# Products of transposed weight strips in two runs per block pair: all high parts, then all low parts

## The chip, the cores and the metric

The kernel runs on one core of one Trainium2 chip. The metric is the device time of one execution in microseconds (us), the median of several executions. The profile is one execution taken by the hardware profiler; its engines are PE (TensorE matmul), PEld (TensorE weight load), DVE (VectorE), ACT (ScalarE), POOL (GpSimd) and SP (SyncE).

## The reference, cut to what matters

A causal decoder trunk with two layers, 256 tokens and a width of 2048, all in float32. Layer 0 has stick-breaking attention with 16 heads; layer 1 has attention over shared keys and values in three dilated groups of four heads. Each layer then has a gated feed-forward part (up to 2 x 5632 columns, a causal convolution of width 3, SiLU gate, down to 2048) and a gated embedding:

```
x = x + mixer(rms_norm(x))                                  # w_qkv, w_o | w_q, w_kv, w_o
u = conv(rms_norm(x) @ w_up);  x = x + (silu(u[:, :D_FF]) * u[:, D_FF:]) @ w_down
x = x + sigmoid(rms_norm(x) @ w_gate) * (p @ w_proj)
```

So nearly all of the work is products of a 256-token activation with large float32 weight matrices that are each used once.

## The kernel before, in words

The stream x is kept transposed: features on the 128 partitions, 256 tokens along the free side, 16 blocks of 128 features. A weight matrix is cut into strips of 512 output columns, and a strip into K-blocks of 128 input features. One load (`L209`, on SP's queue) brings four K-blocks of a strip into a `raw` buffer (1 MB).

Precision comes from splitting each float32 number into a high part that TensorE's reduced float32 type holds exactly and a low part that is the rest. For weights ACT writes the high parts (`whi`, `L217`) and DVE the low parts (`wlo`, `L218`), two K-blocks (a block pair) at a time, into four buffers each. Activations are split the same way and stand as one tile of 512 columns: [high 256 | low 256].

`strip_t` computes four output blocks of 128 features for one strip, transposed, each in a PSUM bank of its own. Per K-block and output block it issues two matmuls on PE, each with a weight load of its own (128 x 128) ahead of it:

- the high product, H: `whi` against all 512 columns of the activation tile, into all 512 columns of the bank. Columns 0 to 255 take high x high, columns 256 to 511 high x low.
- the low product, L: `wlo` against the 256 high columns, added into columns 256 to 511.

In this text an H and its L together are a pair of products. The generator `steps` sets the order: in the first block pair of a strip by output block (so that the new strip can begin as soon as one bank is free), in the middle block by block over the four outputs, and in the last block pair by output again (so that the first output can be read while the others are still computed). In each of these places H and L alternate; only at a strip's very last K-block L stands ahead of H.

There are five such accumulator banks. When an output is complete, ACT copies the second half of its bank out (`L281`) and DVE adds the first half (`L282`), or DVE adds both halves to x (`L289`, `L290`); then the bank is free for the strip after the next output.

`strip_1` (the embedding parts) issues three products of 256 columns per output and block, without a 512-column one. `strip_v` (values) uses the activation as stationary operand and 512 columns of weights as moving one: three products of 512 columns. Both take their order from `steps` too.

A scheduler places the instructions of each engine: it keeps to the program's order where it can, and takes a later instruction first where it reckons that an earlier one would wait. The splitting of weights has a higher priority and runs ahead as far as the four buffers allow. On the chip each engine takes its instructions strictly in that order.

Of the kernel before, what the change touches and what calls it, by code (L numbers as in the profile page):

```python
# [17 lines left out]
P = 128  # L18
S = 256
# [15 lines left out]

# columns of the packed per-feature vectors
G_ATTN, G_FFN, G_PLE, G_KV, G_FIN = 0, 2 * KB, 4 * KB, 6 * KB, 7 * KB
V_CONV = 8 * KB
NVEC = V_CONV + 2 * 4 * 2 * FB
# columns of the packed constants  # L40
C_NT, C_NONE, C_ONE, C_FREQ = 0, P, 2 * P, 3 * P
# [4 lines left out]
TWO_PI = 2.0 * math.pi  # L46
NBANK = {"acc": 5, "att": 1}  # PSUM banks by use; two more are a pair of their own
MAGIC = 1.5 * 2.0 ** 23
# [15 lines left out]

RAW = 4  # K-blocks of a weight load
NRING, NRAW, NWSP = 42, 4, 4  # buffers: K-blocks, weights as loaded, weights split
AHEAD = 200  # how far in the program the splitting of weights may run ahead
LAG = 2  # blocks by which the first norm's squares trail the split
KV_AT = (0, 6, 12, 16)  # blocks split for K and V behind each of the query strips
PI_PARTS = _two_pi_parts()  # L70
# [3 lines left out]
def tile_trunk(ctx, tc, xT_d, pT_d, pos_d, vec_d, cst_d, csb_d, wqkv, wo_a, wkv, wq_b, wo_b, wup, wdn, wpg, wpp, out_d):  # L74
# [28 lines left out]

    # ---- loads of vectors, constants and the stream
    vec = cst.tile([P, NVEC], F32, name="vec")
# [22 lines left out]

    # ---- pieces
    def split_x(src, j, bases):  # L130
        """K-blocks of src * gain, split exactly: [high 256 | low 256]."""
        out = []
        for b in bases:
            h = rt("h", dt=F32R)
            nc.scalar.activation(h[:, :S], src, AF.Copy, scale=gain(b, j))
            nc.vector.scalar_tensor_tensor(  # L136
                h[:, S:], src, gain(b, j), f32(h[:, :S]), op0=OP.mult, op1=OP.subtract
            )
            out.append(h)
        return out  # L140
# [5 lines left out]
    class Norm:  # L146
        """Sum of squares over the blocks as they come, then 1/rms on every partition."""

# [6 lines left out]
        def load_table(self):  # L155
            """The table set with both Ln and Exp, behind what ACT has been given so far."""
            self.table = nc.scalar.preload_act_table_set("natural_log_exp_and_others")
            tc.keep_in_program_order(self.table)
# [40 lines left out]
    def weights(W, s, n, fine=False, before=lambda k0: None, base=0):  # L199
        """Pairs of K-blocks of a strip, split: (first block, high parts, low parts)."""  # L200
        size = 2 if fine else RAW
# [19 lines left out]
    def steps(it, n, outs, tail=2, begin=True):  # L221
        """(block, output, parts) of a strip: by output where outputs begin and in the last blocks."""
        held = []
        for k0, hi, lo in it:
            if k0 >= n - tail:
                held.append((k0, hi, lo))
            elif k0 == 0 and begin:
                yield from ((k0 + i, o, hi[:, i], lo[:, i]) for o in range(outs) for i in range(2))
            else:
                yield from ((k0 + i, o, hi[:, i], lo[:, i]) for i in range(2) for o in range(outs))  # L230
        for o in range(outs):
            yield from ((k0 + i, o, hi[:, i], lo[:, i]) for k0, hi, lo in held for i in range(2))

    def strip_t(W, s, xs, fine=False, before=lambda k0: None, base=0):
        """Four output blocks, transposed: [main | corrections] in a bank each."""
        n = len(xs)
        ps = [None] * 4
        for k, o, hi, lo in steps(weights(W, s, n, fine, before, base), n, 4, begin=not fine):
            if k == 0:
                ps[o] = bank("acc", "acc")  # L240
            c = slice(o * P, (o + 1) * P)
            if k < n - 1:
                nc.tensor.matmul(ps[o], hi[:, c], xs[k], start=k == 0, stop=False)  # L243
                nc.tensor.matmul(ps[o][:, S:], lo[:, c], xs[k][:, :S], start=False, stop=False)  # L244
            else:
                nc.tensor.matmul(ps[o][:, S:], lo[:, c], xs[k][:, :S], start=False, stop=False)  # L246
                nc.tensor.matmul(ps[o], hi[:, c], xs[k], start=False, stop=True)  # L247
        return ps

    def strip_1(W, s, xs, tail=2, two=None):  # L250
        """Four output blocks, transposed, all three products in 256 columns."""
        n = len(xs)
        ps = [None] * 2
        a = dict(skip_group_check=True)
        for k, o, hi, lo in steps(weights(W, s, n), n, 4, tail):
            if k == 0 and o % 2 == 0:
                ps[o // 2] = two[:, o // 2, :] if two is not None else bank("acc", "acc")
            c = slice(o * P, (o + 1) * P)
            d = ps[o // 2][:, (o % 2) * S : (o % 2 + 1) * S]
            nc.tensor.matmul(d, lo[:, c], xs[k][:, :S], start=k == 0 and o % 2 == 0, stop=False, **a)  # L260
            nc.tensor.matmul(d, hi[:, c], xs[k][:, S:], start=False, stop=False, **a)  # L261
            nc.tensor.matmul(d, hi[:, c], xs[k][:, :S], start=False, stop=k == n - 1, **a)  # L262
        return [ps[o // 2][:, (o % 2) * S : (o % 2 + 1) * S] for o in range(4)]

    def strip_v(W, s, xs):
        """512 output columns with the tokens on the partitions."""
        n = len(xs)
        ps = [None] * 2
        for k, t, hi, lo in steps(weights(W, s, n), n, 2):
            if k == 0:  # L270
# [29 lines left out]
    def pv(a0, a1, v, h, o):  # L300
        """o <- (weighted values)^T of a head, split. a0: keys 0 x 256, a1: keys 1 x 128."""
        po = bank("po")
# [4 lines left out]

    # ---- rotary tables: cos and signed sin on 32 partitions
    rot = cst.tile([ROT, 2, S], F32, name="rot")
# [30 lines left out]
    def rotate(t):  # L340
        """t: [128, 256] of a head, in place on its first 32 partitions."""
        sw = tt("sw", (ROT, S), tag="t", bufs=6)
# [4 lines left out]

    # ---- layer parts
    def stick_weights(q, k):
        """Weights^T of two heads a tile: keys 0 x 256 queries of each, keys 1 x 128 of each."""  # L350
        ws = []
# [63 lines left out]
    def mixer_b(hq, hkv_of, rstd, rc):  # L415
# [20 lines left out]
        for g in range(NG):  # L436
            k = project(wkv, g, hkv, None)
            gm = cbf[:, B_GM + g * S : B_GM + (g + 1) * S]
            for h in range(HG):
# [16 lines left out]
                es.append(e)  # L456
        # weights of the groups, from the softmax denominators
        lse = cst.tile([P, 2, NG, HG], F32, name="lse")
# [132 lines left out]

    # ---- the trunk
    idf = cst.tile([P, P], F32, name="idf")
# [43 lines left out]

# ---- layout on the host


def _strips(w):
    """[K, N] -> [N/512, K/512, 128, 4, 512]: four K-blocks of a strip are one run of memory."""
    k, n = w.shape
# [4 lines left out]
def _cols(v):  # L648
    """[..., n * 128] -> [128, ...*n]"""
    return np.ascontiguousarray(v.reshape(-1, P).T)  # L650
# [66 lines left out]
```

## Time and profile before

| | |
|---|---|
| median of three runs | 2414.59 us (2414.16 to 2414.65) |
| span of the profiled execution, first to last instruction | 2413.4 us, 1.2 us below the median |
| PE busy | 2390.6 us (99%), 13914 matmuls and as many weight loads |
| DVE busy | 1645.9 us (68%) |
| ACT busy | 1271.4 us (53%) |
| DMA | 439.92 MB at 182 GB/s over the span |
| chain that ended last | PE 98% |

How to read it: a matmul's row has a start and a duration, but matmuls are pipelined and the next one starts well before the duration of the one before is over. So the durations don't add up to time. What a matmul costs in a dense stretch is the distance from its start to the start of the next one, and that is what this document calls its slot. The weight load rows (PEld) start with the matmul ahead and overlap it.

### The profile page before, as it was taken

The page shows a single profiled execution, that of the slowest core. Times are in us where ns is not written, and L with a number is a line of the kernel's source. Part 1 is how long each engine was busy: PE and PEld are TensorE (multiplying, and loading weights), DVE is VectorE, ACT ScalarE, POOL GpSimd, SP SyncE. Part 2 cuts the span into 40 slices and gives each one's busy share as a digit, 9 for nine tenths or more (in the row PEclk, how much of TensorE's full clock was granted, in tenths as well). Part 3 has the DMA queues.
Part 4 walks back from the last instruction along what each step waited for, and adds up shares of the span by engine and source line. Part 5 has one row for each costly group of instructions (what it writes and reads, how often), then busy time and mean ns, then how long its engine had stood idle before and what let it go on. Part 6 is the DMA issues. An engine that isn't in the chain of part 4 may idle for free.

```text
span 2413.4 us, 34932 instructions
## 1 busy us (share of the span) xinstructions
PE 2390.6 (99%) x13914; PEld 2089.3 (87%) x13914; DVE 1645.9 (68%) x2654; ACT 1271.4 (53%) x1845; POOL 3.6 (0%) x6
## 2 busy tenths in 40 slices
PE   8999999999999999999999999999999999999997
PEld 7888888888888888888998888888888888888897
DVE  8555556777765577766778875777776557776665
ACT  6555545655543455644555444565554345555453
POOL 0000000000000000000000000000000000000000
PEclk9999999999999999999999999999999999999999
DMA  7444445555555555555555444555555555555542
GB/s 277 163 169 170 162 174 197 182 185 191 185 185 189 187 182 190 190 184 186 175 192 184 169 155 166 188 190 189 180 190 191 181 187 192 182 185 192 183 166 105
DMA packets 64004, 439.92 MB, mean 182 GB/s; under 512 B 7232, under 2 KB 7392, under 8 KB 12128
## 3 DMA queue, kind: packets, MB, share of 16 engines
q1 hardware_dynamic: 62352, 435.19, 51.1%
q10 hardware_dynamic: 1488, 2.49, 0.3%
q8 instruction: 109, 1.79, 0.3%
q14 instruction: 55, 0.45, 0.1%
HBM read 435.55 MB, written 2.10 MB: 181 GB/s over the span
## 4 chain that ended last, share of the span: by engine, by line
PE 98%; DVE 1%; ACT 1%; DMA 0%; issue 0%; DVEq 0%; SPq 0%; ACTq 0%
PE acc L243 50%; PE acc L244 25%; PE acc L247 3%; PE acc L262 2%; PE acc L261 2%; PE acc L260 2%; PE accv L274 2%; PE accv L275 2%; PE accv L276 2%; PE acc L246 2%; PE po L304 1%; ACT whi L217 0%; DVE wlo L218 0%; PE two L260 0%; PE two L261 0%; PE two L262 0%
## 5 line engine op out<-in xcount | busy, mean ns | idle before, releaser
L218 DVE TENSOR_TENSOR wlo<-raw,whi 128x1024 fp32r<-128x1024 f32 (+1 forms) x825 | 1007.6, 1222 | 677.5 <-ACT whi L217 672.4
L217 ACT ACTIVATE whi<-raw 128x1024 fp32r<-128x1024 f32 (+1 forms) x825 | 871.8, 1058 | 930.4 <-PE acc L243 691.8
L243 PE MATMUL acc<-h,whi 128*128 128x512 f32 x3480 | 1241.7, 399 | 8.6 <-DVE h L136 8.6
L244 PE MATMUL acc<-h,wlo 128*128 128x256 f32 x3480 | 977.2, 281 | 0.0
L243 PEld LDWEIGHTS acc<-h,whi 128*128 128x128 f32 x3480 | 655.2, 188 | 158.3 <-DVE h L136 8.6
L244 PEld LDWEIGHTS acc<-h,wlo 128*128 128x128 f32 x3480 | 658.2, 189 | 10.4
L243 PE MATMUL acc<-g,whi 128*128 128x512 f32 x1344 | 476.0, 398 | 0.0
L244 PE MATMUL acc<-g,wlo 128*128 128x256 f32 x1344 | 375.5, 280 | 0.0
L243 PEld LDWEIGHTS acc<-g,whi 128*128 128x128 f32 x1344 | 252.3, 188 | 58.8
L244 PEld LDWEIGHTS acc<-g,wlo 128*128 128x128 f32 x1344 | 253.7, 189 | 3.3
L243 PE MATMUL acc<-o,whi 128*128 128x512 f32 x416 | 147.9, 398 | 0.0
L262 PE MATMUL acc<-h,whi 128*128 128x256 f32 x512 | 145.3, 284 | 0.0
L260 PE MATMUL acc<-h,wlo 128*128 128x256 f32 x512 | 144.9, 283 | 0.0
L261 PE MATMUL acc<-h,whi 128*128 128x256 f32 x512 | 144.9, 283 | 0.0
L244 PE MATMUL acc<-o,wlo 128*128 128x256 f32 x416 | 115.2, 280 | 0.0
L281 ACT ACTIVATE c<-acc 128x256 f32<-128x256 f32 x232 | 86.4, 373 | 30.5 <-PE acc L247 30.5
L261 PEld LDWEIGHTS acc<-h,whi 128*128 128x128 f32 x512 | 98.2, 192 | 0.1
L262 PEld LDWEIGHTS acc<-h,whi 128*128 128x128 f32 x512 | 98.2, 192 | 0.1
L260 PEld LDWEIGHTS acc<-h,wlo 128*128 128x128 f32 x512 | 98.2, 192 | 0.1
L282 DVE TENSOR_TENSOR c<-acc,c 128x256 f32<-128x256 f32 x232 | 91.8, 416 | 0.7 <-ACT c L281 0.7
L247 PE MATMUL acc<-h,whi 128*128 128x512 f32 x232 | 92.0, 397 | 0.0
L243 PEld LDWEIGHTS acc<-o,whi 128*128 128x128 f32 x416 | 77.9, 188 | 16.0
(164 smaller groups left out, 2014.5 us busy)
## 6 DMA issues: line engine op xcount, KB each, us to landing
raw<-in_wup SPq DMA_DIRECT2D x176, 1024.0 KB, 4.8
raw<-in_wdn SPq DMA_DIRECT2D x88, 1024.0 KB, 4.8
raw<-in_wqkv SPq DMA_DIRECT2D x44, 1024.0 KB, 4.8
raw<-in_wpg SPq DMA_DIRECT2D x32, 1024.0 KB, 4.8
raw<-in_wkv SPq DMA_DIRECT2D x24, 1024.0 KB, 4.8
raw<-in_wo_a SPq DMA_DIRECT2D x16, 1024.0 KB, 4.8
raw<-in_wq_b SPq DMA_DIRECT2D x12, 1024.0 KB, 4.8
raw<-in_wo_b SPq DMA_DIRECT2D x12, 1024.0 KB, 4.8
```

The lines of the kernel that those rows point to most:

```text
L217: nc.scalar.activation(hi[:, c], r, AF.Copy)
L218: nc.vector.tensor_tensor(lo[:, c], r, f32(hi[:, c]), op=OP.subtract)
L243: nc.tensor.matmul(ps[o], hi[:, c], xs[k], start=k == 0, stop=False)
L244: nc.tensor.matmul(ps[o][:, S:], lo[:, c], xs[k][:, :S], start=False, stop=False)
L246: nc.tensor.matmul(ps[o][:, S:], lo[:, c], xs[k][:, :S], start=False, stop=False)
L247: nc.tensor.matmul(ps[o], hi[:, c], xs[k], start=False, stop=True)
L260: nc.tensor.matmul(d, lo[:, c], xs[k][:, :S], start=k == 0 and o % 2 == 0, stop=False, **a)
L261: nc.tensor.matmul(d, hi[:, c], xs[k][:, S:], start=False, stop=False, **a)
L262: nc.tensor.matmul(d, hi[:, c], xs[k][:, :S], start=False, stop=k == n - 1, **a)
L274: nc.tensor.matmul(ps[t], xl, hi, start=k == 0, stop=False)
L281: nc.scalar.activation(c, ps[:, S:], AF.Copy)
L282: nc.vector.tensor_tensor(c, ps[:, :S], c, op=OP.add)
```

## The change

`steps` now yields lists (groups) of products where it yielded single ones: a group for each output in a strip's first and last block pair, and one group of eight (four outputs, two blocks) for each block pair in the middle. `strip_t` takes a group and issues all H of it, and then all L. The last L of an output now ends its accumulation. In the very first strip of the program the first group is sorted by block. `strip_1` and `strip_v` flatten the groups; their middle block pairs now go output by output with the two blocks side by side, where they went block by block. Comments were removed as well.

```diff
     def steps(it, n, outs, tail=2, begin=True):
...
             elif k0 == 0 and begin:
-                yield from ((k0 + i, o, hi[:, i], lo[:, i]) for o in range(outs) for i in range(2))
+                for o in range(outs):
+                    yield [(k0 + i, o, hi[:, i], lo[:, i]) for i in range(2)]
             else:
-                yield from ((k0 + i, o, hi[:, i], lo[:, i]) for i in range(2) for o in range(outs))
+                yield [(k0 + i, o, hi[:, i], lo[:, i]) for o in range(outs) for i in range(2)]
         for o in range(outs):
-            yield from ((k0 + i, o, hi[:, i], lo[:, i]) for k0, hi, lo in held for i in range(2))
+            yield [(k0 + i, o, hi[:, i], lo[:, i]) for k0, hi, lo in held for i in range(2)]
 
     def strip_t(W, s, xs, fine=False, before=lambda k0: None, base=0):
...
-        for k, o, hi, lo in steps(weights(W, s, n, fine, before, base), n, 4, begin=not fine):
-            if k == 0:
-                ps[o] = bank("acc", "acc")
-            c = slice(o * P, (o + 1) * P)
-            if k < n - 1:
+        for group in steps(weights(W, s, n, fine, before, base), n, 4, begin=not fine):
+            if fine and group[0][0] == 0:
+                group.sort(key=lambda g: g[0])
+            for k, o, hi, lo in group:
+                if k == 0:
+                    ps[o] = bank("acc", "acc")
+                c = slice(o * P, (o + 1) * P)
                 nc.tensor.matmul(ps[o], hi[:, c], xs[k], start=k == 0, stop=False)
-                nc.tensor.matmul(ps[o][:, S:], lo[:, c], xs[k][:, :S], start=False, stop=False)
-            else:
-                nc.tensor.matmul(ps[o][:, S:], lo[:, c], xs[k][:, :S], start=False, stop=False)
-                nc.tensor.matmul(ps[o], hi[:, c], xs[k], start=False, stop=True)
+            for k, o, hi, lo in group:
+                c = slice(o * P, (o + 1) * P)
+                nc.tensor.matmul(ps[o][:, S:], lo[:, c], xs[k][:, :S], start=False, stop=k == n - 1)
         return ps
```

How the instructions move. The first place is PE's order for one middle block pair of a strip of the down projection (`g` are its activation blocks, `acc` the banks, 512 columns mark an H and 256 an L). Before:

```order
L243 MATMUL acc_6099<-g_6051,whi_6309 128x512
L244 MATMUL acc_6099<-g_6051,wlo_6310 128x256
L243 MATMUL acc_6104<-g_6051,whi_6309 128x512
L244 MATMUL acc_6104<-g_6051,wlo_6310 128x256
L243 MATMUL acc_6109<-g_6051,whi_6309 128x512
L244 MATMUL acc_6109<-g_6051,wlo_6310 128x256
```

And the same block pair now, up to its third L:

```order
L246 MATMUL acc_6099<-g_6051,whi_6309 128x512
L246 MATMUL acc_6099<-g_6064,whi_6309 128x512
L246 MATMUL acc_6104<-g_6051,whi_6309 128x512
L246 MATMUL acc_6104<-g_6064,whi_6309 128x512
L246 MATMUL acc_6109<-g_6051,whi_6309 128x512
L246 MATMUL acc_6109<-g_6064,whi_6309 128x512
L246 MATMUL acc_6114<-g_6051,whi_6309 128x512
L246 MATMUL acc_6114<-g_6064,whi_6309 128x512
L249 MATMUL acc_6099<-g_6051,wlo_6310 128x256
L249 MATMUL acc_6099<-g_6064,wlo_6310 128x256
L249 MATMUL acc_6104<-g_6051,wlo_6310 128x256
```

Eight H now stand in a row, and the eight L (three are shown) behind them; the two blocks of the pair go into a bank one directly behind the other.

The second place is the end of that strip and the start of the next one on PE. Before, from the last output's last three products on:

```order
L244 MATMUL acc_6114<-g_6077,wlo_6330 128x256
L246 MATMUL acc_6114<-g_6090,wlo_6330 128x256
L247 MATMUL acc_6114<-g_6090,whi_6329 128x512
L243 MATMUL acc_6363<-g_3871,whi_6359 128x512
L244 MATMUL acc_6363<-g_3871,wlo_6360 128x256
L243 MATMUL acc_6363<-g_3884,whi_6359 128x512
L244 MATMUL acc_6363<-g_3884,wlo_6360 128x256
```

Now, the same stretch:

```order
L246 MATMUL acc_6114<-g_6090,whi_6329 128x512
L249 MATMUL acc_6114<-g_6077,wlo_6330 128x256
L249 MATMUL acc_6114<-g_6090,wlo_6330 128x256
L246 MATMUL acc_6363<-g_3871,whi_6359 128x512
L246 MATMUL acc_6363<-g_3884,whi_6359 128x512
L249 MATMUL acc_6363<-g_3871,wlo_6360 128x256
L249 MATMUL acc_6363<-g_3884,wlo_6360 128x256
```

At strip ends and starts the runs are two long: H H L L for each output, where an end had H L L H and a start H L H L.

The third place lies a few rows on, where the new strip's fourth output (`acc_6378`) begins. Before, its products stood directly behind the third output's, ahead of the second block pair (`whi_6383`):

```order
L244 MATMUL acc_6373<-g_3884,wlo_6360 128x256
L243 MATMUL acc_6378<-g_3871,whi_6359 128x512
L244 MATMUL acc_6378<-g_3871,wlo_6360 128x256
L243 MATMUL acc_6378<-g_3884,whi_6359 128x512
L244 MATMUL acc_6378<-g_3884,wlo_6360 128x256
L243 MATMUL acc_6363<-g_3897,whi_6383 128x512
```

Now:

```order
L249 MATMUL acc_6373<-g_3884,wlo_6360 128x256
L246 MATMUL acc_6363<-g_3897,whi_6383 128x512
L246 MATMUL acc_6363<-g_3910,whi_6383 128x512
L246 MATMUL acc_6368<-g_3897,whi_6383 128x512
L246 MATMUL acc_6378<-g_3871,whi_6359 128x512
L246 MATMUL acc_6378<-g_3884,whi_6359 128x512
L249 MATMUL acc_6378<-g_3871,wlo_6360 128x256
```

The scheduler here took three H of the second block pair ahead of the fourth output's first product, so the second block pair's high parts are asked for four products earlier.

Over the whole program there are as many matmuls, weight loads, splits, evictions and DMAs as before. Of the 5568 H of `strip_t`, 4264 stand in middle block pairs, in runs of eight, and 1304 in strips' first and last block pairs, in runs of two; near some strip starts the scheduler made runs of five and three of them. SP's queue is unchanged; on DVE and ACT some evictions and splits change places with their neighbours.

More of the change, by code (lines that the diff above doesn't have):

```diff
@@ L254, in strip_1 @@
         a = dict(skip_group_check=True)
-        for k, o, hi, lo in steps(weights(W, s, n), n, 4, tail):
+        for k, o, hi, lo in (g for group in steps(weights(W, s, n), n, 4, tail) for g in group):
             if k == 0 and o % 2 == 0:
@@ L268, in strip_v @@
         ps = [None] * 2
-        for k, t, hi, lo in steps(weights(W, s, n), n, 2):
+        for k, t, hi, lo in (g for group in steps(weights(W, s, n), n, 2) for g in group):
             if k == 0:
```

## The prediction

> **What bounds the kernel now.** I read the page first: busy shares, granted clock, chain.
>
> ```profile
> PE 2390.6 (99%) x13914; PEld 2089.3 (87%) x13914; DVE 1645.9 (68%) x2654; ACT 1271.4 (53%) x1845; POOL 3.6 (0%) x6
> PEclk9999999999999999999999999999999999999999
> PE 98%; DVE 1%; ACT 1%; DMA 0%; issue 0%; DVEq 0%; SPq 0%; ACTq 0%
> PE acc L243 50%; PE acc L244 25%; PE acc L247 3%; PE acc L262 2%; PE acc L261 2%; PE acc L260 2%; PE accv L274 2%; PE accv L275 2%; PE accv L276 2%; PE acc L246 2%; PE po L304 1%; ACT whi L217 0%; DVE wlo L218 0%; PE two L260 0%; PE two L261 0%; PE two L262 0%
> ```
>
> The chain lies on PE for 98% of the span, and 80% of it are the lines of `strip_t` (50 + 25 + 3 + 2). The granted clock stays at nine tenths or more (1.00 in the windows below). Then PE's waits:
>
> ```profile
> PE acc L243 <- DVE h L136: 8.6, 1, 8.6
> PE nrm L176 <- ACT sq L165: 1.1, 2, 0.7
> ```
>
> The first matmul waits 8.6 us for its activation; after that hardly anything is waited for. PE is therefore bound by how fast it takes matmuls, and the change can only act through the slots of H and L, from one start to the next. How many there are, from the groups of PE kept apart by shape:
>
> ```profile
> L243 PE MATMUL acc<-h,whi 128*128 128x512 f32 x3480 | 1241.7, 399 | 8.6 <-DVE h L136 8.6
> L243 PE MATMUL acc<-g,whi 128*128 128x512 f32 x1344 | 476.0, 398 | 0.0
> L243 PE MATMUL acc<-o,whi 128*128 128x512 f32 x416 | 147.9, 398 | 0.0
> L247 PE MATMUL acc<-h,whi 128*128 128x512 f32 x232 | 92.0, 397 | 0.0
> L247 PE MATMUL acc<-g,whi 128*128 128x512 f32 x64 | 25.4, 396 | 0.0
> L247 PE MATMUL acc<-o,whi 128*128 128x512 f32 x32 | 12.7, 396 | 0.0
> ```
>
> That is 5240 + 328 = 5568 pairs of an H and an L. The mean durations (399 ns) overlap, so I don't add them; the price of a pair comes from long dense windows. Window, its length, PE busy and matmuls of L243, and below of L247, in two stretches of the up projections:
>
> ```profile
> 430.00:670.00 240.00, 227.78 (x641) 1.00 0.54 189
> 1572.00:1816.00 244.00, 231.78 (x653) 1.00 0.53 186
> ...
> 430.00:670.00 240.00, 15.88 (x40) 1.00 0.54 189
> 1572.00:1816.00 244.00, 15.88 (x40) 1.00 0.53 186
> ```
>
> 240 / 681 = 0.3524 us and 244 / 693 = 0.3521 us a pair. I take 0.3522, and for the whole 5568 x 0.3522 = 1961 us, 81% of the span, as the chain has it.
>
> **The change part by part.** It removes and adds no instruction. What it changes is the neighbours of each matmul, so I looked for what a slot costs by its neighbours. In the timeline of PE, alternating order does not have one price. Two stretches, the first and the last row of each:
>
> ```profile
> 500.06 0.40 PE L243 MATMUL acc<-h,whi 128*128 128x512 f32 x1
> 505.37 0.40 PE L243 MATMUL acc<-h,whi 128*128 128x512 f32 x1
> ...
> 1127.75 0.39 PE L243 MATMUL acc<-g,whi 128*128 128x512 f32 x1
> 1133.99 0.39 PE L243 MATMUL acc<-g,whi 128*128 128x512 f32 x1
> ```
>
> The first holds 15 pairs: 5.31 / 15 = 0.354 us. The second holds 18: 6.24 / 18 = 0.3467 us. The same two instructions alternate in both, so PE has a slow and a fast pattern of alternation. 0.3522 lies at about (0.3522 - 0.3467) / (0.354 - 0.3467) = 75% slow. Now slots without alternation, which the other two kinds of strip give. 512 columns behind 512 in `strip_v`, where the first row comes right behind two matmuls of 256:
>
> ```profile
> 227.45 0.39 PE L275 MATMUL accv<-wlo,h 128*128 128x512 f32 x1
> 229.29 0.39 PE L274 MATMUL accv<-whi,h 128*128 128x512 f32 x1
> 231.56 0.39 PE L275 MATMUL accv<-wlo,h 128*128 128x512 f32 x1
> ```
>
> The first eight slots take 1.84 us, 0.230 each; the next ten 2.27 us, 0.227 each. And 256 columns behind 256 in `strip_1`, first behind an H, then deep inside:
>
> ```profile
> 1148.58 0.28 PE L260 MATMUL acc<-h,wlo 128*128 128x256 f32 x1
> 1149.52 0.28 PE L262 MATMUL acc<-h,whi 128*128 128x256 f32 x1
> ...
> 1200.05 0.28 PE L260 MATMUL two<-p,wlo 128*128 128x256 f32 x1
> 1203.89 0.28 PE L262 MATMUL acc<-h,whi 128*128 128x256 f32 x1
> ```
>
> The first eight take 0.94 us, 0.1175 each; the 32 inside 3.84 us, 0.120 each. Settled, an H and an L cost 0.227 + 0.120 = 0.347 us, the fast pattern of alternation. Right after a switch an H is about 3 ns dearer and an L 2.5 ns cheaper, so a run of eight H behind L and a run of eight L behind H cost 1.84 + 0.94 = 2.78 us, or **0.3475 a pair**. The slow pattern shows in no run of equal matmuls.
>
> The 1304 pairs in runs of two have their nearest rows in strip ends, where L L and H H stand side by side:
>
> ```profile
> 604.41 0.28 PE L244 MATMUL acc<-h,wlo 128*128 128x256 f32 x1
> 604.53 0.28 PE L246 MATMUL acc<-h,wlo 128*128 128x256 f32 x1
> 604.65 0.40 PE L247 MATMUL acc<-h,whi 128*128 128x512 f32 x1
> 604.88 0.40 PE L243 MATMUL acc<-h,whi 128*128 128x512 f32 x1
> 606.97 0.40 PE L243 MATMUL acc<-h,whi 128*128 128x512 f32 x1
> ```
>
> From 604.88 to 606.97 there are three outputs with two pairs each: 2.09 / 6 = **0.3483 a pair**. As a circle H L L H and H H L L have the same neighbours, so I take this price.
>
> The sum: 4264 x 0.3475 + 1304 x 0.3483 = 1481.7 + 454.2 = 1935.9 us against 1961, **25.1 us less**. The profiled span of 2413.4 becomes 2388.3; with the 1.2 us by which the median lies above it, 2389.5 us.
>
> Bounds of the pair price, which no row shows in exactly the new order. From below: every pair at 0.3467 gives 1930.4, a gain of 30.6 (2384.0); if all L in the runs kept the cheap 0.1175 beside a settled H of 0.227, 0.3445, it would be 4264 x 0.0077 + 1304 x 0.0039 = 38 us (2376.7), which I hold for unlikely since the rows pay one against the other. From above: the single slots inside `strip_t` itself, L to L 0.12 (604.41 to 604.53) and H to H 0.23 (604.65 to 604.88), make 0.350: 1948.8, a gain of 12.2 (2402.4). Further up lies the slow pattern, a rival.
>
> Edits that I cost at nothing. *Buffers of the split weights*: the H of a block pair are now done eight L earlier, so ACT may refill `whi` about 8 x 0.12 = 1 us sooner; `wlo` comes free at the end of the pair as before.
>
> ```profile
> ACT whi L217 <- PE acc L243: 691.8, 434, 2.6
> DVE wlo L218 <- ACT whi L217: 672.4, 522, 5.2
> ```
>
> ACT already waits for PE, and DVE for ACT, so splitting is ahead and stays hidden; without that cover a pair of splits would cost PE the 1.2 us of a `wlo`. *Banks*: the first output of a new strip takes the fifth bank, and the fourth needs the old third one, read last by this row of DVE:
>
> ```profile
> 607.87 0.41 DVE L282 TENSOR_TENSOR c<-acc,c 128x256 f32<-128x256 f32 x1
> ...
> 609.08 0.40 PE L243 MATMUL acc<-h,whi 128*128 128x512 f32 x1
> ```
>
> It ends at 608.28, 0.8 us ahead of the fourth output. Ends and starts keep their order by output, so this margin stays, and the evictions that changed places on DVE stay within it. *First strip*: each second block's activation is needed behind one to four H instead of four pairs, about 1.2 us sooner.
>
> ```profile
> 20.77 0.47 DVE L136 SCALAR_TENSOR_TENSOR h<-x,vec,h 128x256 fp32r<-128x256 f32 x1
> ...
> 22.44 0.40 PE L243 MATMUL acc<-h,whi 128*128 128x512 f32 x1
> ```
>
> This second block is ready at 21.24, the pair starts at 22.44: still 1.2 us to spare; the 8.6 us at the start stay.
>
> **The rivals.**
>
> *A slot depends on its own columns alone.* Then order is worth nothing: 2414.6. The Trainium skill has such a rule (TensorE: Matmul & The Clock Gate, Back-to-back issue gap): a warm matmul takes N / 2.4 ns and about 2.5 ns more, 325 ns for a pair in any order. Against it stand 0.354 and 0.3467 for the same alternation, and a 512-column slot of 0.230 behind 256 columns and 0.227 later.
>
> *Single-switch prices hold.* If in short runs the 0.350 of the neighbours within `strip_t` stays, the gain is half: 2402.4. For it: these are the only rows with this code's own operands. Against: they are single slots next to an alternating stretch, and each is rounded to 10 ns.
>
> *Slower: the slow pattern takes hold of everything.* If it comes from the ratio of H to L on PE and not from the switching, and the short disorder at strip ends is what now resets it, then runs without such a reset would stand at 0.354 throughout: 5568 x 0.354 = 1971, 10 us more, 2424.6. It decides once more than 75% of the pairs run that way. Against it: `strip_1` and `strip_v` settle at the low price and keep it.
>
> *Slower: the second block pair is asked for too soon.* At a strip's start the scheduler puts H of the second block pair ahead of the fourth output, so PE, in order, would stand there until `whi` is written: up to the two pairs by which it is asked for earlier, 0.7 us, in 82 strips, 57 us, less the 25: 2446. It decides when the split is less than two pairs ahead; ACT's 691.8 us of waiting for PE speak against it.
>
> **How the numbers follow.** The forecast, 2389.5, has 0.68 with everything from 2380 to 2398; half the gain (2402) 0.14; no change 0.07; the slow pattern 0.05; the late block pair 0.04; below 2380 0.02. What a measurement of this kernel can tell from no change is about 0.2%, 4.8 us. Faster by more has 0.68 + 0.14 + 0.02 = 0.84, no change 0.07, slower 0.09. The range goes from 2380 (the 30.6 us gain and a little more) to 2406 (half the gain with its rounding), which leaves out about 0.18.
>
> **What would show it.** In the profile after, the distance from one run of eight H to the next should be 2.77 to 2.80 us in the up projections, where eight alternating pairs take 2.82 now; slots inside runs should be 0.227 to 0.236 and 0.117 to 0.120. PE's wait list should stay as short, with the first 8.6 us unchanged. A distance of 2.83 would be the slow pattern; single long slots at a strip's start the late block pair; 2.80 without such slots half the gain. The prediction is wrong if PE's matmuls start at less than these rates while nothing is waited for, or if the activations of the first strip come late.

## The result

The changed kernel takes 2397.88 us (median of four executions, 2397.71 to 2398.34) against 2414.38 us of the kernel before in the same sessions (2413.18 to 2414.65): a ratio of 0.9932, 95% interval 0.9918 to 0.9946. It is 16.5 us faster; 25.1 us had been forecast. The profiled span is 2396.5 us, 16.9 us shorter.

From the page of the changed kernel: the busy shares and the chain, which answer to the first rows of the prediction.

```profile
PE 2373.7 (99%) x13914; PEld 2091.5 (87%) x13914; DVE 1651.2 (69%) x2654; ACT 1277.0 (53%) x1845; POOL 3.6 (0%) x6
...
PE 98%; DVE 1%; ACT 0%; DMA 0%; issue 0%; DVEq 0%; SPq 0%; ACTq 0%
PE acc L246 54%; PE acc L249 27%; PE acc L264 2%; PE acc L262 2%; PE acc L263 2%; PE accv L277 2%; PE accv L276 2%; PE accv L278 2%; PE po L306 1%; PE two L262 0%; PE two L264 0%; PE two L263 0%; PE two L364 0%; PE two L448 0%; PE po L307 0%; DMA x<-in_xT 0%
```

And what PE waited for in the changed kernel:

```profile
PE acc L246 <- DVE h L136: 9.0, 1, 9.0
PE nrm L176 <- ACT sq L165: 1.1, 2, 0.7
```

PE is the bound as before, on the chain for 98%, with the same two waits. Nothing new is waited for, and nothing that was waited for has gone; the first matmul came 0.3 us later in this execution. So the 17 us came out of the slots.

The timeline of PE in the changed kernel, where neighbouring matmuls of one line are merged into a row with their count. As much as one whole strip of an up projection: the end of the strip before and this one's start, in runs of two from 578.19 on, then this one's six middle block pairs in runs of eight from 583.76 to 600.52. Rows marked ... are left out.

```profile
578.19 0.63 PE L246 MATMUL acc<-h,whi 128*128 128x512 f32 x2
578.66 0.39 PE L249 MATMUL acc<-h,wlo 128*128 128x256 f32 x2
...
583.76 2.00 PE L246 MATMUL acc<-h,whi 128*128 128x512 f32 x8
585.60 1.12 PE L249 MATMUL acc<-h,wlo 128*128 128x256 f32 x8
586.56 2.00 PE L246 MATMUL acc<-h,whi 128*128 128x512 f32 x8
...
600.52 0.63 PE L246 MATMUL acc<-h,whi 128*128 128x512 f32 x2
```

Sixteen pairs in runs of two take 5.57 us, 0.348 each; 48 pairs in runs of eight take 16.76 us, 0.3492 each. The whole strip has 22.33 / 64 = 0.3489 us a pair where the kernel before had 0.3522. Times 5568 pairs that is 18 us, the gain as near as windows of this length give it. The distance from one run of eight H to the next is 16.76 / 6 = 2.793 us, between the 2.77 and 2.80 that the prediction named as its sign.

### The profile page after: what moved, and what is told of

The parts are those of the page before. It is cut to its first block, busy times and chain, and to the rows that moved or that the text cites. A ratio compares the mean times of both kernels' runs of the same rounds, so it can differ in the third digit from the quotient of the medians.

```text
span 2396.5 us, 35018 instructions
## 1 busy us (share of the span) xinstructions
PE 2373.7 (99%) x13914; PEld 2091.5 (87%) x13914; DVE 1651.2 (69%) x2654; ACT 1277.0 (53%) x1845; POOL 3.6 (0%) x6
## 4 chain that ended last, share of the span: by engine, by line
PE 98%; DVE 1%; ACT 0%; DMA 0%; issue 0%; DVEq 0%; SPq 0%; ACTq 0%
PE acc L246 54%; PE acc L249 27%; PE acc L264 2%; PE acc L262 2%; PE acc L263 2%; PE accv L277 2%; PE accv L276 2%; PE accv L278 2%; PE po L306 1%; PE two L262 0%; PE two L264 0%; PE two L263 0%; PE two L364 0%; PE two L448 0%; PE po L307 0%; DMA x<-in_xT 0%
## 5 line engine op out<-in xcount | busy, mean ns | idle before, releaser
L246 PE MATMUL acc<-h,whi 128*128 128x512 f32 x3712 | 993.3, 394 | 9.0 <-DVE h L136 9.0
L246 PEld LDWEIGHTS acc<-h,whi 128*128 128x128 f32 x3712 | 643.0, 189 | 99.3 <-DVE h L136 9.0
L249 PEld LDWEIGHTS acc<-h,wlo 128*128 128x128 f32 x3712 | 554.4, 190 | 67.9
L249 PE MATMUL acc<-h,wlo 128*128 128x256 f32 x3712 | 573.2, 282 | 0.0
L246 PE MATMUL acc<-g,whi 128*128 128x512 f32 x1408 | 369.3, 393 | 0.0
L249 PEld LDWEIGHTS acc<-g,wlo 128*128 128x128 f32 x1408 | 205.2, 190 | 22.6
L249 PE MATMUL acc<-g,wlo 128*128 128x256 f32 x1408 | 210.9, 281 | 0.0
L262 PE MATMUL acc<-h,wlo 128*128 128x256 f32 x512 | 144.9, 283 | 0.0
L246 PE MATMUL acc<-o,whi 128*128 128x512 f32 x448 | 121.3, 394 | 0.0
L264 PEld LDWEIGHTS acc<-h,whi 128*128 128x128 f32 x512 | 98.3, 192 | 0.1
L262 PEld LDWEIGHTS acc<-h,wlo 128*128 128x128 f32 x512 | 98.3, 192 | 0.1
L263 PEld LDWEIGHTS acc<-h,whi 128*128 128x128 f32 x512 | 98.3, 192 | 0.0
L277 PE MATMUL accv<-wlo,h 128*128 128x512 f32 x224 | 88.6, 395 | 0.0
L276 PE MATMUL accv<-whi,h 128*128 128x512 f32 x224 | 88.5, 395 | 0.0
L278 PE MATMUL accv<-whi,h 128*128 128x512 f32 x224 | 87.9, 392 | 0.0
```

What stands on the lines that cost most here:

```text
L276: nc.tensor.matmul(ps[t], xl, hi, start=k == 0, stop=False)
L277: nc.tensor.matmul(ps[t], xh, lo, start=False, stop=False)
L278: nc.tensor.matmul(ps[t], xh, hi, start=False, stop=k == n - 1)
```

## The experiments

Each was timed beside the kernel before on the same chip. "Round" below is one run of H with the run of L behind it; 346.7 ns is the settled price of a pair (226.7 + 120): the price deep inside a run, where a slot no longer changes. Code cuts show the lines that matter; ... marks what is left out. A pattern of alternation is called fast at 0.3467 us a pair and slow at 0.3533; where pairs are counted as fast or slow, the count is taken from the starts of all of a trace's matmuls, in groups of three alternating pairs (1.04 us fast, 1.06 slow).

**Is it the runs, or the grouping by output?** The change did two things at once: it made runs, and it put the two blocks of an output side by side. First the grouping alone, from the kernel before:

```diff
-                yield from ((k0 + i, o, hi[:, i], lo[:, i]) for i in range(2) for o in range(outs))
+                yield from ((k0 + i, o, hi[:, i], lo[:, i]) for o in range(outs) for i in range(2))
```

> Only the order of groups is changed: middle block pairs go output by output with the two blocks side by side, but H and L still alternate, and a strip's end is as before. If the gain of 16.5 us comes from the runs, alternation keeps its slow pattern (three pairs in 1.06 us) and this stands at 2414 us, as before. If it comes from the grouping by output (both blocks into one bank one behind the other), it stands near 2398 us.

Measured: 2414.77 us, ratio 0.9998 (0.9989 to 1.0007). Then the runs alone, from the changed kernel:

```diff
-                yield [(k0 + i, o, hi[:, i], lo[:, i]) for o in range(outs) for i in range(2)]
+                yield [(k0 + i, o, hi[:, i], lo[:, i]) for i in range(2) for o in range(outs)]
```

> The changed kernel with its runs of eight, but inside a run first the four outputs of one block, then those of the other (the order by block that the kernel before had). If the runs do it: 2398 us, 8 H and 8 L in 2.793 us as in the changed kernel. If the grouping by output does it: back to about 2414 us.

Measured: 2397.97 us, ratio 0.9931 (0.9918 to 0.9943). Its timeline of PE has the same rounds, two of them in 5.59 us:

```profile
499.81 2.00 PE L246 MATMUL acc<-h,whi 128*128 128x512 f32 x8
501.65 1.11 PE L249 MATMUL acc<-h,wlo 128*128 128x256 f32 x8
502.61 2.00 PE L246 MATMUL acc<-h,whi 128*128 128x512 f32 x8
...
505.40 0.86 PE L246 MATMUL acc<-h,whi 128*128 128x512 f32 x3
```

The runs do all of it; into which bank or from which block neighbouring products go makes no difference.

**What a round costs.** If a round has a price of its own, the time depends on how long the runs are. Three kernels change the length of the middle's runs. Runs of two:

```diff
-                yield [(k0 + i, o, hi[:, i], lo[:, i]) for o in range(outs) for i in range(2)]
+                for o in range(outs):
+                    yield [(k0 + i, o, hi[:, i], lo[:, i]) for i in range(2)]
```

> The changed kernel with middle block pairs in runs of two (H H L L for each output) as at strip ends. Settling theory: a round of switches costs more the further the L run has settled; the strip ends of the changed kernel show 2.786 us for eight pairs in runs of two against 2.793 in runs of eight, so 4264 x (349.1 - 348.3 ns) = about 3 us less than the changed kernel: 2395 us. Rival, each round of switches costs the same 20 ns: 346.7 + 20/2 = 356.7 ns a pair, 2430 us.

Measured: 2395.76 us, ratio 0.9921 (0.9907 to 0.9934). Seven rounds of its timeline:

```profile
499.81 0.63 PE L247 MATMUL acc<-h,whi 128*128 128x512 f32 x2
500.28 0.39 PE L250 MATMUL acc<-h,wlo 128*128 128x256 f32 x2
...
504.69 0.63 PE L247 MATMUL acc<-h,whi 128*128 128x512 f32 x2
```

4.88 us for 14 pairs, 0.3486 each. Runs of four:

```diff
-                yield [(k0 + i, o, hi[:, i], lo[:, i]) for o in range(outs) for i in range(2)]
+                for i in range(2):
+                    yield [(k0 + i, o, hi[:, i], lo[:, i]) for o in range(outs)]
```

> The changed kernel with middle block pairs in runs of four (four H of one block, its four L). Settling theory: of the slots that the changed kernel shows behind a switch, the first four H are together 23 ns over the settled 226.7 and the first four L 7.5 under 120, 16 ns for four pairs: 350.6 ns a pair, 4264 x 1.5 ns = 6 us more than the changed kernel, 2404 us, dearer than runs of two and of eight. Rival, the cost falls or rises evenly with the run's length: between the price of runs of two (348.3 ns) and of eight (349.1), 2396 to 2397 us.

Measured: 2406.53 us, ratio 0.9967 (0.9954 to 0.9979). Three rounds of its timeline:

```profile
500.26 1.09 PE L247 MATMUL acc<-h,whi 128*128 128x512 f32 x4
501.19 0.63 PE L250 MATMUL acc<-h,wlo 128*128 128x256 f32 x4
...
504.46 0.86 PE L247 MATMUL acc<-h,whi 128*128 128x512 f32 x3
```

4.20 us for 12 pairs, 0.350 each. Runs of sixteen, two block pairs joined in one group:

```diff
...
-                yield [(k0 + i, o, hi[:, i], lo[:, i]) for o in range(outs) for i in range(2)]
+                mid.append((k0, hi, lo))
+                if len(mid) == wide or k0 + 2 >= n - tail:
+                    yield [(k + i, o, h[:, i], l[:, i]) for o in range(outs) for k, h, l in mid for i in range(2)]
+                    mid = []
...
```

`wide` is two block pairs, and one in the very first strip of the program.

> The changed kernel with two middle block pairs joined, runs of 16 H and 16 L. Settling theory: the 20 ns of a round are paid once in 16 pairs, 347.9 ns a pair instead of 349.1: about 5 us less than the changed kernel, 2393 us, unless the low parts of the second block pair come late or the split buffers (four of each, of which a group now holds two) make PE wait, which would show in its wait list. If the price depended on something else than the switches: 2398 us.

Measured: 2394.28 us, ratio 0.9915 (0.9901 to 0.9928). One round of its timeline:

```profile
505.01 3.82 PE L249 MATMUL acc<-h,whi 128*128 128x512 f32 x16
508.67 2.08 PE L252 MATMUL acc<-h,wlo 128*128 128x256 f32 x16
510.58 0.63 PE L249 MATMUL acc<-h,whi 128*128 128x512 f32 x2
```

5.57 us for 16 pairs, 0.348 each. The order of prices is the one that settling gives: 2 cheaper than 8, 4 dearer than both, 16 the cheapest (2395.8, 2397.9, 2406.5, 2394.3 us). A cost that grew or fell evenly with the length, or one that is the same for each round, is out. The traces also show where a round's cost lies. In the changed kernel's rounds the single slots of H, averaged over some 500 rounds from the starts in the trace, are 233, 236, 228, 232, 231 and then three times 227 ns, together 27 ns over the settled price; those of L are 113, 119 and then six times 120 ns, 8 ns under it. So a round of eight costs 20 ns over the settled price (2793 ns against 2773), paid by the first five H behind a settled run of L. Counted in the same way, a round of two costs 3 ns over the settled price, a round of four 16 and a round of sixteen 20: runs of two never let the L settle, runs of four pay most of the price for half the pairs, and runs of sixteen pay it half as often. The runs of four came out 2.5 us above the 2404 expected, although their rounds cost 0.3507 us a pair where 0.3506 had been expected; where the rest lies stays open.

**Which part of a strip carries the gain.** Runs in the middle alone, with strips beginning in H L H L and ending in H L L H as before:

```diff
                 for o in range(outs):
-                    yield [(k0 + i, o, hi[:, i], lo[:, i]) for i in range(2)]
+                    for i in range(2):
+                        yield [(k0 + i, o, hi[:, i], lo[:, i])]
...
+            if group[0][0] == n - 1:
+                ((k, o, hi, lo),) = group
+                c = slice(o * P, (o + 1) * P)
+                nc.tensor.matmul(ps[o][:, S:], lo[:, c], xs[k][:, :S], start=False, stop=False)
+                nc.tensor.matmul(ps[o], hi[:, c], xs[k], start=False, stop=True)
+                continue
...
```

> Only the middle block pairs in runs of eight; strips begin with H L H L and end with H L L H for each output as before. If the slow pattern of alternation in the middle is where the time was, nearly the whole gain is here: 2398 to 2400 us. If the ends carried a part in proportion to their number of pairs (1304 of 5568, 23%): 2402 us.

Measured: 2402.79 us, ratio 0.995 (0.9938 to 0.9963), 4.9 us slower than the changed kernel. On top of the runs in the middle, those at the ends bring this part of the 16.5 us, a share a little above their number (1304 of 5568 pairs, 23%). Then runs at the ends alone, with an alternating middle:

```diff
-                yield [(k0 + i, o, hi[:, i], lo[:, i]) for o in range(outs) for i in range(2)]
+                for i in range(2):
+                    for o in range(outs):
+                        yield [(k0 + i, o, hi[:, i], lo[:, i])]
```

> Only a strip's first and last block pair in runs of two; the middle alternates as before. If the middle's slow pattern is where the time was: 2413 us or a little more, at most 2 us less than before. If the ends carry their share by number: 2410.5 us. If H H L L at a strip's start leaves alternation in the fast pattern (346.7 ns a pair), the middle gains too: 4264 x 6.6 ns, up to 2386 us.

Measured: 2402.54 us, ratio 0.9955 (0.9942 to 0.9969). Its executions lie between 2401.2 and 2405.7. This is 12 us of gain from the ends alone, far more than their share, though less than an entirely fast middle would give. Windows of this kernel, with their length and the number of H:

```profile
450.00:700.00 250.00, 244.44 (x711) 1.00 0.54 187
760.00:1040.00 280.00, 273.42 (x807) 1.00 0.55 190
1580.00:1830.00 250.00, 243.97 (x711) 1.00 0.54 186
1860.00:2180.00 320.00, 312.87 (x923) 1.00 0.55 190
```

In the first and third window a pair takes 250 / 711 = 0.3516 us, in the second 280 / 807 = 0.3470 and in the fourth 320 / 923 = 0.3467. (A window also counts the matmuls that its edges cut, so such a price can come out some tenths of a per cent low.) The instructions are of the same two shapes in all four. Alternation here holds one pattern, slow or fast, over hundreds of pairs and across the ends of strips: 684 alternating pairs between 428 and 737 us are slow, and 696 between 744 and 1054 us fast. It changes at some strip's start.

**Does it come from mixing two lengths?** The kernel before with every L as wide as an H (low x low is computed too, so there is more work):

```diff
-                nc.tensor.matmul(ps[o][:, S:], lo[:, c], xs[k][:, :S], start=False, stop=False)
+                nc.tensor.matmul(ps[o], lo[:, c], xs[k], start=False, stop=False)
             else:
-                nc.tensor.matmul(ps[o][:, S:], lo[:, c], xs[k][:, :S], start=False, stop=False)
+                nc.tensor.matmul(ps[o], lo[:, c], xs[k], start=False, stop=False)
```

> The kernel before with every L made as wide as an H: the low weights against all 512 columns of the activation, so that low x low is added too, and the slots that alternate are of one length. If the slow pattern comes from mixing slots of two lengths, both settle at 226.7 ns: 453.3 ns a pair, 5568 x (453.3 - 352.0) = 564 us more, 2978 us. If it comes from alternating between the buffers of high and low weights, the 6.6 ns a pair stay: 460 ns, 3015 us.

Measured: 2976.8 us, one execution. Windows of this kernel by its main H line, and below by the H of strips' last blocks:

```profile
600.00:800.00 200.00, 161.13 (x415) 1.00 0.43 148
...
600.00:800.00 200.00, 10.50 (x27) 1.00 0.43 148
```

200 / 442 = 0.4525 us a pair, twice the settled 226.7 ns as near as the window gives it. The high and low weights still alternate, each with a weight load of its own, and there is no slow pattern. So alternating the weights is not enough for it. That the two lengths are what it needs is the nearest reading, but the edit also lets an L read all of the activation tile and write the whole bank instead of its second half, and that was not tried apart from the length.

**What decides between the fast and the slow pattern.** First alternation without any break: the kernel before with H ahead of L at a strip's last block too.

```diff
-            if k < n - 1:
-                nc.tensor.matmul(ps[o], hi[:, c], xs[k], start=k == 0, stop=False)
-                nc.tensor.matmul(ps[o][:, S:], lo[:, c], xs[k][:, :S], start=False, stop=False)
-            else:
-                nc.tensor.matmul(ps[o][:, S:], lo[:, c], xs[k][:, :S], start=False, stop=False)
-                nc.tensor.matmul(ps[o], hi[:, c], xs[k], start=False, stop=True)
+            nc.tensor.matmul(ps[o], hi[:, c], xs[k], start=k == 0, stop=False)
+            nc.tensor.matmul(ps[o][:, S:], lo[:, c], xs[k][:, :S], start=False, stop=k == n - 1)
```

> The kernel before with H ahead of L at a strip's last block too, so that H and L alternate without a break from a strip's first product to its last (before, each strip ended with H L L H for each output). The kernel with runs of two at the ends alone showed alternation keep its pattern, fast or slow, over hundreds of pairs and across strip ends, and change it only at some of them. If the pattern is a state that lasts until something upsets it, long stretches in one pattern show here, of either kind, and the time lies anywhere from 2384 (all fast) to 2421 us (all slow), away from 2414. If each strip's end in H L L H has nothing to do with it, every strip turns slow after its first pairs as before: 2414 us.

Measured: 2401.03 us as a median, ratio 0.9937 (0.9923 to 0.995), but its executions lie between 2390.6 and 2402.2, while those of the runs of sixteen stay within 0.8 us. The profiled execution is the 2390.6, and two of its windows are fast:

```profile
430.00:690.00 260.00, 260.00 (x752) 1.00 0.55 190
1560.00:1820.00 260.00, 260.00 (x751) 1.00 0.55 191
```

260 / 752 = 0.346 us a pair (0.3467 from one start to the next). The same execution has slow stretches too: 108 pairs from 93.8 to 131.6 us start 0.3533 us apart. In all 1616 of its 1807 groups are fast and 132 slow. With nothing at strip ends to break it, alternation mostly stays in whichever pattern it is in. That the slower executions had more slow stretches is inferred: 11.6 us more would be about 1760 of the 5568 pairs at 6.6 ns; only the fastest one was profiled.

Then one unit H H L L in the third block pair, with alternation around it and the ends in runs of two. The cut is against the kernel with runs at the ends alone:

```diff
+                if k0 == 4:
+                    yield [(k0 + i, 0, hi[:, i], lo[:, i]) for i in range(2)]
                 for i in range(2):
-                    for o in range(outs):
+                    for o in range(1 if k0 == 4 else 0, outs):
                         yield [(k0 + i, o, hi[:, i], lo[:, i])]
```

> The kernel with runs of two at strip ends alone, with one more unit H H L L in the third block pair of each strip, alternation around it. In that kernel alternation turned fast where the last unit's low slots were 116 and 112 ns long and slow where they were 113 and 119 ns. If one unit turns the one into the other, the stretches that were slow (428 to 744 us, 1059 to 1119, 1565 to 1848) become fast and the fast ones slow, or a slow entry is cut off in each strip: a time away from 2402.5 us, down to 2388 if each strip leaves the unit in the fast pattern. If the unit does nothing lasting, 2402 to 2403 us.

Measured: 2405.63 us, ratio 0.9963 (0.995 to 0.9975). It is slower than without the unit, so the hoped-for exchange of whole stretches did not come, but the strips show what a unit does. One strip of its timeline:

```profile
563.35 0.40 PE L250 MATMUL acc<-h,whi 128*128 128x512 f32 x1
...
566.12 0.62 PE L250 MATMUL acc<-h,whi 128*128 128x512 f32 x2
566.59 0.40 PE L253 MATMUL acc<-h,wlo 128*128 128x256 f32 x2
566.82 0.40 PE L250 MATMUL acc<-h,whi 128*128 128x512 f32 x1
...
574.24 0.40 PE L250 MATMUL acc<-h,whi 128*128 128x512 f32 x1
```

Ahead of the unit at 566.12 there are 8 pairs in 2.77 us, 0.346 each; behind it 21 pairs in 7.42 us, 0.353 each. A single unit of four products turned the fast pattern into the slow one. Of the 49 such units in this trace with fast alternation ahead of them, 48 have slow alternation behind; of 11 with slow alternation ahead, 7 stay slow and 4 turn fast.

Then alternation entered from a settled run of H, by pairing the L of each block pair with the H of the next:

```diff
...
+            if len(group) == 8:
+                for j, g in enumerate(group):
+                    if late:
+                        low(*late[j])
+                    high(*g)
+                late = group
+                continue
+            for g in late:
+                low(*g)
...
```

`high` and `low` issue one H and one L; `late` holds the block pair whose L are still to come.

> The changed kernel's groups, but in the middle of a strip the eight L of a block pair alternate with the eight H of the next one: eight H alone, then L and H in turn, and eight L alone before the strip's last block pair. Alternation is entered in every strip from a settled run of H. If what alternation costs is decided by how it is entered, all strips go one way, and executions agree within about 1 us: either fast, 4264 x (349.1 - 346.7 ns) = 10 us less than the changed kernel less about 1.6 us for 82 rounds of 20 ns, so 2389 us; or slow, 4264 x (353.3 - 349.1) = 18 us more and the same 1.6 us, 2417 us. If the entry decides nothing, strips of both kinds stand side by side and the time lies between, with executions some us apart as where H and L alternate without a break.

Measured: 2410.09 us, ratio 0.998 (0.9971 to 0.9989), its executions within 1.2 us. Its timeline, twelve pairs of one strip's middle:

```profile
564.79 0.28 PE L245 MATMUL acc<-h,wlo 128*128 128x256 f32 x1
565.25 0.40 PE L242 MATMUL acc<-h,whi 128*128 128x512 f32 x1
...
569.49 0.40 PE L242 MATMUL acc<-h,whi 128*128 128x512 f32 x1
```

4.24 us for the twelve pairs from 565.25 on, 0.3533 each, and so in nearly every strip: over the whole execution 1000 of 1161 groups are slow and 76 fast. The entry decides, and this entry is a slow one. The 2417 us expected had an error: 656 of the pairs stand in the runs at the start and the end of the middle and not in alternation; counted rightly it is 3608 x 353.3 + 656 x 346.7 + 82 x 20 ns = 1503.7 us against 1488.6, 2413 us. Most of the other 3 us are the strips that were not slow: the alternating pairs of this execution average 352.6 ns instead of 353.3, which is 2.5 us for 3608 pairs.

**An entry that is nearly always fast.** In the changed kernel the first unit H H L L behind a run of eight L has low slots of about 116 and 112 ns, the next one of about 113 and 119, in all 80 places where the two follow each other. In the kernels with runs at the ends alone and with the extra unit, units of both kinds stand ahead of alternation: behind 97 of the first kind it was fast each time, behind 106 of the second kind slow each time. The low slots are a mark by which the two can be told apart, not a cause. So the last kernel builds such an entry in every strip: one block pair in runs of eight, one unit, then alternation; the ends stay in runs of two.

```diff
-                yield [(k0 + i, o, hi[:, i], lo[:, i]) for o in range(outs) for i in range(2)]
+                if k0 <= 2:
+                    yield [(k0 + i, o, hi[:, i], lo[:, i]) for o in range(outs) for i in range(2)]
+                    continue
+                if k0 == 4:
+                    yield [(k0 + i, 0, hi[:, i], lo[:, i]) for i in range(2)]
+                for i in range(2):
+                    for o in range(1 if k0 == 4 else 0, outs):
+                        yield [(k0 + i, o, hi[:, i], lo[:, i])]
```

> The changed kernel with the first middle block pair of each strip in runs of eight, then one unit H H L L, then alternation to the strip's end. In the changed kernel the first unit H H L L behind a settled run of L always has low slots of 116 and 112 ns, and alternation turned fast behind such a unit in the other runs. If the entry decides and the pattern lasts, every strip is fast in its middle: 656 pairs at 349.1 and 3608 at 346.7 ns instead of 4264 at 349.1, 9 us less than the changed kernel: 2389 us, the same within about 1 us in every execution. If the pattern is chance, strips of both kinds show and the time lies between 2389 and 2413 us, with executions some us apart. If every entry by a given order ends slow as with the skewed one, 2413 us.

Measured: 2389.89 us (2388.81 to 2390.61), ratio 0.9898 (0.9881 to 0.9914): 25 us faster than the kernel before and 8 us faster than the changed one. Its timeline, the entry and the alternation behind it:

```profile
561.32 1.12 PE L256 MATMUL acc<-h,wlo 128*128 128x256 f32 x8
562.27 0.63 PE L253 MATMUL acc<-h,whi 128*128 128x512 f32 x2
562.74 0.39 PE L256 MATMUL acc<-h,wlo 128*128 128x256 f32 x2
562.97 0.40 PE L253 MATMUL acc<-h,whi 128*128 128x512 f32 x1
563.32 0.39 PE L253 MATMUL acc<-h,whi 128*128 128x512 f32 x1
...
569.21 0.40 PE L253 MATMUL acc<-h,whi 128*128 128x512 f32 x1
```

Seventeen pairs from 563.32 to 569.21 take 5.89 us, 0.3465 each. Over the whole execution 1048 of 1094 groups are fast and 38 slow, where the kernel before has 208 of 1548 fast and 1308 slow. This is the fastest kernel of the case, and its time repeats. Whether the run of eight would do it alone, with alternation directly behind it, was not tried.

## Why the prediction was right, and where its size was off

**Right: the bound and the place.** PE's slots set the time, the waits are unchanged, and the price of a pair fell. Time and sign lie within what was forecast: 2397.9 is inside the range, and inside the band up to 2398 that the forecast had for itself by 0.1 us only, which is luck.

**Right: two patterns of alternation, mostly slow.** 0.354 against 0.3467 was read from the kernel before, and the slow one did not come up in runs. Forcing it one way by the entry gives 2389.9 and 2410.1 us. The share was read too low, though: three quarters slow came from 0.354, the price in one short stretch; the slow pattern has 0.3533, and 1308 of 1548 groups, 84%, are slow. No term of the sum used the share.

**Right: the runs of two.** 0.3483 had been taken from strip ends; 0.348 was measured.

**Mis-sized: the term 4264 x 0.3475.** Runs of eight cost 0.3492, so this term was 4264 x 1.7 ns = 7 us too low, nearly all of the 8.6 us by which the gain fell short. The step that failed put together two rows that don't occur together. The eight 512-column products (1.84 us) stood behind only two of 256 columns, and the eight 256-column ones (0.94 us) behind the end of a strip, L L H, not behind a settled run of H. From the starts in the trace the two rows are 1838 and 946 ns; in a real round the eight H take 1841 and the eight L 952. So the H were nearly right, and most of the miss is in the L: in a real round they gain 8 ns on the settled price, in the row taken they gained 14. The sentence that "the rows pay one against the other" was half true: the H pay 27 ns, the L give back 8. Together the two rows lie 9 ns under a real round, about 5 us in the kernel; the other 2 us are rounding, since 1838 and 946 were read as 1.84 and 0.94, 4 ns lower in sum. Of the remaining 1.6 us, 0.8 is the price before (0.3522 from windows, about 0.3520 from all starts, leaving out the few long waits) and 0.3 the first matmul, which came later.

**Rivals.** That a slot depends on its own columns alone is refuted: the same matmuls give 2389.9 to 2410.1 us by order. The slow pattern did not take hold in runs, and the block pair asked for earlier was never late: PE's waits are the same. The single-switch price, 0.350 a pair, was not so far off for runs of eight (0.3492), but by luck: it is not the price of a switch, since runs of two switch four times as often and cost less.

**What the edits at nothing cost.** Nothing that shows: no wait of PE on banks, splits or the first strip's second blocks has come up. That ACT and DVE are still ahead is in the changed kernel's waits (engine, line, what it waited for, total, times, longest):

```profile
ACT whi L217 <- PE acc L246: 694.9, 504, 2.7
DVE wlo L218 <- ACT whi L217: 662.3, 511, 5.1
```

## What to carry to other kernels

Where a dense stretch of matmuls bounds a kernel, read the distance between starts over several repeats of the exact order, not the duration of a row or two rows from different surroundings; a price put together from neighbours that never met was off by half of a per cent here, and that was over a quarter of the gain forecast. Look for stretches in which the same instructions run at two rates, since the better one is a target. A few products in another order at the right place can be worth more than reordering everything: runs at each strip's ends and start, with alternation left in the rest of the middle, gave 25 us, the full reordering 16.5.

## What the hardware showed that was not expected

- Alternating matmuls of 512 and 256 columns, as this kernel issues them, run in one of two patterns, 0.3467 or 0.3533 us a pair, at the same granted clock (1.00) and with nothing waited for. The pattern lasts over hundreds of pairs, and four products in another order can turn the fast one into the slow one. Long runs of one length settle at 226.7 and 120 ns a slot here.
- Behind a settled run of 256-column matmuls the first five of 512 columns are 27 ns dearer together; behind a settled run of 512-column ones the first two of 256 columns are 8 ns cheaper.
- Unbroken alternation, the simplest order, varied from 2390.6 to 2402.2 us between executions of one kernel, and alternation with runs at the ends alone from 2401.2 to 2405.7, where the two kernels with alternation behind a settled run (of H, or of L with one unit) stayed within 2 us each. What differs between those executions at the point of entry was not seen.
- Why there are two patterns stays open. The runs show that the entry decides, and one execution speaks for two lengths being needed; no view shows what inside PE, its weight loads or its reads is out of step.
